# One more pair of output tiles as seven products in three places of a hybrid decoder layer

## The chip, the cores and the metric

The kernel runs on one core of a Trainium2 chip. A core has five engines, each with an instruction queue of its own that it works off in order: TensorE (PE, matrix products into PSUM, with PEld for the loading of its stationary operand), VectorE (DVE), ScalarE (ACT), GpSimd (POOL) and SyncE (SP, which here issues the DMAs). The engines run beside one another and wait for one another by semaphores. The metric is the device time of one execution in microseconds, and of several runs the median. A lower time is better.

## The reference

One layer step for 512 prompt tokens, 32 new tokens of running sequences and 16 meta tokens (560 columns in all; 544 once the meta tokens have done their part), width 1024, FFN width 2816:

```python
h = x + 0.5 * rms_norm(swiglu(rms_norm(x, ffn1_pre_g), ffn1_w_gate, ffn1_w_up, ffn1_w_down), ffn1_post_g)
u = rms_norm(h, mix_pre_g)
q_a, k_a, v_a, gk_low, r_a, q_b, k_b, v_b, gate_a, gate_b = jnp.split(u @ w_in, offs, axis=-1)
o_a = rms_norm(gla(q_a, k_a, v_a, gk_low), gla_norm_g) * jax.nn.silu(r_a)
o_b = stick_breaking_attention(q_b, k_b, v_b, sb_bias)
m = jax.nn.sigmoid(gate_a) * (o_a @ w_o_gla) + jax.nn.sigmoid(gate_b) * (o_b @ w_o_sb)
h = h + rms_norm(m @ w_out, mix_post_g)
y = h + 0.5 * rms_norm(swiglu(rms_norm(h, ffn2_pre_g), ffn2_w_gate, ffn2_w_up, ffn2_w_down), ffn2_post_g)
```

with `swiglu(x, g, u, d) = (silu(x @ g) * (x @ u)) @ d`, all in float32.

## The kernel before, in words

Everything lies feature-major: a tile has 128 features on the partitions and the tokens along the row, in two halves of 280 columns (272 once the meta tokens are gone). The 1024 features are 8 depth tiles, the 2816 of the FFN 22.

**A product in three matmuls.** Each float32 operand is split in two parts of fp32r: `hi`, a cast on ACT (`S.copy`), and `lo`, the value less `hi`, a subtraction on DVE (`tt` with `ALU.subtract`, whose instructions all carry line 166). A depth tile of a product is then hi times hi, hi times lo and lo times hi, for each half: 6 matmuls. A tile of 8 depth tiles takes 48.

**Seven products in place of eight.** Two output tiles over eight depth tiles, with two halves of columns, are a 2 x 2 by 2 x 2 product of quarters. They are also computed as seven products (PLAN and MIXER call such a pair "S" and a plain tile "R"): 7 x 4 x 3 = 84 matmuls in place of 96. For this DVE makes four sums of weight quarters (`weight_sums`, four of 128x512) and splits the quarters and sums of weights in four parts (`parts_of`, `parted_lo`: b1, t and b2 of 128x1024, t4 of 128x512), and four sums of activations s1 to s4 for each k of 0 to 3 (four instructions of half a row each), which are split as well; afterwards some adds put the seven results together. `seven_steps` does this for the mixer, `Down.pair` for the FFN's down projections.

**The order.** PE, DVE, ACT and POOL have a written-out order. `step()` marks every six matmuls, and `later(n, f)` puts `f` behind the n-th step from here on its engine's queue; `when` does so with steps counted from a pair's start. Nothing in that fixes a time: it fixes who stands behind whom. SP's order is a scheduler's. The rooms in SBUF are given out by the table PLACES, one byte for each `take`.

**FFN and down projection.** In the FFN (lines 1075 to 1306) gate and up are computed for tile f = 0 to 21; `hidden` splits the product of the two in `hi` and `lo` for the down projection. Tiles up to `late` are split as they come; from LATE (8) on they wait unsplit in `waiting`, and are split in every second step after the FFN's last matmul. Then follows the down projection, class `Down` and the loop over `by_chunks(order)`. Before, output tiles 0 and 1 are computed plainly, by turns in three chunks of depth (0 to 7, 8 to 14, 15 to 21), 44 steps and 264 matmuls in all. Then come the pairs 2 and 4: each plainly over the depth tiles 8 to 21 (`CUTS`, 28 steps, 168 matmuls, L1391 to L1394), and over the depth tiles 0 to 7 as seven products (84 matmuls, L1430 to L1432), the results being added to the plain ones. Tiles 6 and 7 follow plainly, one half after the other. For the activation sums `joined` puts `hi` and `lo` of depth tile i and i + 4 together again, `summed` makes s1 to s4, `sums_hi` and `sums_lo` split them; `pieces` queues all this for i = 0 to 3 from step DSUMS[0] on, every DSUMS[1] steps.

**The mixer's r gate.** `chain` runs the mixer's products by the table MIXER, its first ones beside the last pairs of heads of the attention. r has eight tiles: r 0, 1, 2 and 7 plain (`gate_r`, a tile of eight depth tiles in `tile_steps`, L699 to L702), then the pairs 3 and 5 as seven products (`r_pair`). `sums_back`, `sums_hi` and `sums_lo` make the activation sums for the mixer's pairs, at the steps SUMS_BACK; `whole_u` adds `hi` and `lo` of u for this, `halved` gives back rooms that only plain tiles need, and `out_a` is the product with w_o_gla, whose first tile names its depth order as the o tiles come ready.

Of the kernel before, what the change touches and what calls it, by code (L numbers as in the profile page):

```python
# [35 lines left out]
LATE1, LATE2 = 8, 8  # L36
# [20 lines left out]
6806666991008264690078680607082491770776681c069186424e3e343a74546e7266323c00368c4468767c2840781e6c820c0238708c762a2e
26927c8a040660622a2c4816246527702e1262186071152c622a2b2d6415712c1262632a622a2b2d642c71626306180c1e62714b71246a003254
883e64604b38020434308a6058763c786222122a482e4c4a8e2c7b84668c687e7f406056464f3d333579036b366e747044426c7215015939318b
7782893f055514157a804e5a7e825c2483284e655e92647c508d3a521e148c822667648466616764656766422c7016604668746c6e647244206a  # L60
0a6612088a6c1804343c8c780688916a761a720f026e22320e1c103057565584641486544000760c676a6c8a7248082e604c1a3e582a910e2c66
301c856e001257421002685655542040164675150c8a146a0a300e121e188c782a2c007074107620060421863442736c6e728988846475668e0c
17343e12324c4a42460b7476486a3c1c3004436e20080972621a3736876660860a436c8417686e8e6a642c1488568c430408063c906394708417
6664606c6e78728e8a68846a86606e17708468646a6c7894728e668a0c866e606c176478686a848e728a66706e6c866072177084026836646a6c
8e00786686948a6e401c6620721a1e178a646030948e106c0c6a0e181c2068708486366e786a4072102a221e20170094667038840e1a6e8e0c1c
60724068641c8a1e1a186c220260206e8e59540e2a0c84721e302e68100066606c94641e3840202200706694308e8464606e4740721002682e0e
# [68 lines left out]
def hybrid_step(  # L135
# [570 lines left out]
    def k_steps(acc, parts, k0, k1, kt, act, halves, nw=P, wid=(HW, HW)):  # L706
        hi, lo = parts
        for k in range(k0, k1):
# [15 lines left out]

    def step():

        arena.now += 1
        n = 0
# [2021 lines left out]
```

## Time and profile before

| | before |
|---|---|
| median of 3 runs | 1492.89 us (1492.89 to 1494.05) |
| the profiled execution | 1493.21 us |
| its span | 1491.2 us |
| granted clock of PE | 0.999 |
| PE instructions, matmuls and transposes | 11909 |
| DVE, ACT, POOL busy | 1106.0, 783.1, 68.4 us |
| DMA | 181.97 MB, mean 122 GB/s |

The span goes from the first to the last instruction that the profile shows; the execution's own time has 2.0 us besides. Times in the trace count from the span's start. A matmul row lists the modelled end, so that successive rows overlap: one of 128x280 is listed with 0.29 us, and the next starts 0.13 later.

The stages by the trace: FFN1's gate and up to 266.35, its down projection to 401, projections and GLA to 580, attention to 820, the mixer from 806 to 1056, w_out to 1143, FFN2's gate and up to 1347.95, its down projection to 1480, and the end.

### The profile page before, as it was taken

Reading aid. Unit: us, or ns where it says so; the run is one execution under the profiler, and the core shown is the slowest. Engines: PE = TensorE matmul, PEld = TensorE weight load, DVE = VectorE, ACT = ScalarE, POOL = GpSimd, SP = SyncE. Lnnn points to the kernel's source line nnn. Section 1 sums busy time; section 2 is a strip of 40 time slices with the busy share of each in tenths; the row PEclk is TensorE's granted clock in tenths of the full one; section 3 lists DMA queues with packets and bytes.
Section 4 is the critical chain, followed back from the end, with each engine's and each line's share of the span. In section 5 each row is a group of like instructions: output and inputs, shape, how many; then the busy total and the mean of one; then the engine's idle time right before and its main releaser. Section 6 shows DMA issues by size and latency. Waiting matters only on the chain.

```text
span 1491.2 us, 29865 instructions
## 1 busy us (share of the span) xinstructions
PE 1482.6 (99%) x11909; PEld 1435.2 (96%) x11909; DVE 1106.0 (74%) x1945; ACT 783.1 (53%) x1453; POOL 68.4 (5%) x145
## 2 busy tenths in 40 slices
PE   9999999999999999999999999999999999999998
PEld 8999999999999899999998999999999999999998
DVE  5888888855677866877887845777567898888544
ACT  7455454533555656566666543634564455455333
POOL 2000000000000011112111000000000000000000
PEclk9999999999999999999999999999999999999999
DMA  8133333324665584336555866344531333333253
GB/s 253 50 92 100 100 96 92 97 79 123 172 153 138 148 151 100 86 95 161 125 112 160 228 162 200 96 110 140 155 111 52 100 100 100 99 107 92 79 152 115
DMA packets 277230, 181.97 MB, mean 122 GB/s; under 512 B 10429, under 2 KB 255363, under 8 KB 277091
## 3 DMA queue, kind: packets, MB, share of 16 engines
q1 hardware_dynamic: 276786, 180.00, 44.7%
q8 instruction: 93, 1.52, 0.4%
q14 instruction: 47, 0.38, 0.1%
q0 software_dynamic: 288, 0.07, 0.0%
q10 hardware_dynamic: 16, 0.00, 0.0%
HBM read 155.06 MB, written 24.97 MB: 121 GB/s over the span
## 4 chain that ended last, share of the span: by engine, by line
PE 96%; DVE 2%; ACT 1%; DMA 1%; issue 0%; DVEq 0%; ACTq 0%
PE acc L1266 8%; PE acc L1267 8%; PE acc L1268 8%; PE acc L699 7%; PE acc L700 7%; PE acc L702 7%; PE acc L712 6%; PE acc L715 6%; PE acc L713 6%; PE acc L1046 2%; PE acc L1047 2%; PE acc L1048 2%; PE acc L1209 2%; PE acc L1206 2%; PE acc L1207 2%; PE ps L2041 1%
## 5 line engine op out<-in xcount | busy, mean ns | idle before, releaser
L166 DVE TENSOR_TENSOR room<-room,room 128x544 f32<-128x544 f32 (+18 forms) x457 | 285.6, 648 | 72.3 <-ACT room L779 16.7
L166 DVE TENSOR_TENSOR lo<-raw,hi 128x1024 fp32r<-128x1024 f32 (+1 forms) x207 | 248.1, 1199 | 105.5 <-ACT hi L678 66.7
L1266 PE MATMUL acc<-room,hi 128*128 128x280 f32 (+1 forms) x896 | 260.0, 290 | 0.0
L1268 PE MATMUL acc<-room,lo 128*128 128x280 f32 (+1 forms) x896 | 259.6, 290 | 0.0
L1267 PE MATMUL acc<-room,hi 128*128 128x280 f32 (+1 forms) x896 | 259.4, 289 | 0.0
L699 PE MATMUL acc<-room,hi 128*128 128x280 f32 x832 | 241.1, 307 | 0.2 <-DVE room L169 0.2
L700 PE MATMUL acc<-room,hi 128*128 128x280 f32 x832 | 225.0, 289 | 0.0
L977 ACT CAST hi<-raw 128x1024 fp32r<-128x1024 f32 x100 | 104.8, 1052 | 146.2 <-PE acc L1267 48.6
L702 PE MATMUL acc<-room,lo 128*128 128x280 f32 x832 | 173.1, 289 | 0.0
L1267 PEld LDWEIGHTS acc<-room,hi 128*128 128x128 f32 x896 | 168.9, 188 | 0.0
L1266 PEld LDWEIGHTS acc<-room,hi 128*128 128x128 f32 x896 | 168.8, 188 | 0.0
L1268 PEld LDWEIGHTS acc<-room,lo 128*128 128x128 f32 x896 | 168.6, 188 | 0.0
L699 PEld LDWEIGHTS acc<-room,hi 128*128 128x128 f32 x832 | 156.8, 188 | 10.1 <-issue 8.1
L700 PEld LDWEIGHTS acc<-room,hi 128*128 128x128 f32 x832 | 157.2, 189 | 1.2
L678 ACT CAST hi<-raw 128x1024 fp32r<-128x1024 f32 (+1 forms) x107 | 108.2, 1013 | 75.2 <-issue 21.5
L702 PEld LDWEIGHTS acc<-room,lo 128*128 128x128 f32 x832 | 130.3, 189 | 0.0
L977 ACT CAST hi<-room 128x1024 fp32r<-128x1024 f32 x92 | 76.9, 836 | 87.3 <-PE acc L1267 58.5
L166 DVE TENSOR_TENSOR lo<-room,hi 128x1024 fp32r<-128x1024 f32 x92 | 87.9, 955 | 43.4 <-ACT hi L977 43.0
L712 PE MATMUL acc<-room,hi 128*128 128x280 f32 (+2 forms) x388 | 110.8, 295 | 0.0
L713 PE MATMUL acc<-room,hi 128*128 128x280 f32 (+2 forms) x388 | 108.9, 290 | 0.0
L166 DVE TENSOR_TENSOR room<-room,acc 128x272 f32<-128x272 f32 (+1 forms) x180 | 76.2, 437 | 43.8 <-PE acc L1048 20.9
L712 PE MATMUL acc<-room,room 128*128 128x280 f32 (+3 forms) x364 | 107.4, 295 | 0.0
(397 smaller groups left out, 3437.2 us busy)
## 6 DMA issues: line engine op xcount, KB each, us to landing
raw<-in_w_in_dram SPq DMA_DIRECT2D x43, 512.0 KB, 7.2
raw<-in_ffn_w_gate_dram SPq DMA_DIRECT2D x64, 256.0 KB, 3.1
raw<-in_ffn_w_up_dram SPq DMA_DIRECT2D x64, 256.0 KB, 3.4
raw<-in_ffn_w_down_dram SPq DMA_DIRECT2D x36, 448.0 KB, 3.9
raw<-in_w_in_dram SPq DMA_DIRECT2D x40, 256.0 KB, 4.7
out_dram<-room SPq DMA_DIRECT2D x36, 256.0 KB, 3.7
room<-in_cache_k_dram SPq DMA_DIRECT2D x32, 256.0 KB, 5.7
room<-in_cache_v_dram SPq DMA_DIRECT2D x32, 256.0 KB, 4.7
```

Source lines behind the costliest of these rows:

```text
L166: (eng or V).tensor_tensor(out=out, in0=a, in1=b, op=op)
L678: S.copy(h_, src)
L699: T.matmul(acc[h][:, : wid[h]], hi[k], a[h][0], start=(k == order[0]), stop=False)
L700: T.matmul(acc[h][:, : wid[h]], hi[k], a[h][1], start=False, stop=False)
L702: T.matmul(acc[h][:, : wid[h]], lo[k], a[h][0], start=False, stop=(k == order[-1]))
L712: T.matmul(acc[h][:nw, : wid[h]], wh, a[h][0], start=(k == 0), stop=False)
L713: T.matmul(acc[h][:nw, : wid[h]], wh, a[h][1], start=False, stop=False)
L715: T.matmul(acc[h][:nw, : wid[h]], wl, a[h][0], start=False, stop=(k == kt - 1))
L977: S.copy(hi[:, :kt], src)
L1266: T.matmul(x[:, :QW], hi, act[k][0], start=(first and k == 0), stop=False, skip_group_check=True)
L1267: T.matmul(x[:, :QW], hi, act[k][1], start=False, stop=False, skip_group_check=True)
L1268: T.matmul(x[:, :QW], lo, act[k][0], start=False, stop=(k == 3), skip_group_check=True)
```

## The change

In each down projection the tiles 0 and 1 are no longer computed plainly: pair 0 is done as the pairs 2 and 4 are. In all three pairs the plain part is now over the depth tiles 0 to 13 (`CUTS`) and the seven products over 14 to 21 (`S0` = 14), the last eight that the FFN makes. The tiles from 14 on are kept unsplit until they have been summed, so that `joined` goes: `summed` reads them from `hid.wait`, `parted` splits them at the side, `given` gives their rooms back. `first` splits the tiles 12 and 13, LATE goes from 8 to 12, so that 8 to 11 are split inside the FFN, and the activation sums start at step 1, every 6 steps, in place of 14 and 8. The seven products now begin 28 steps after the projection's first matmul; before it was 44 + 28.

In the mixer the plain r tiles 2 and 7 go, and r is 0 and 1 plain, then the pairs 2, 4 and 6. SUMS_BACK, `halved` and the depth order of the first `out_a` follow. `um.full` has another layout for k below 4, which costs `whole_u` one add more. PSUM tags are exchanged, and PLACES is a new table, of which one line each is shown. In the whole program PE has 36 matmuls fewer, DVE 25 instructions more, ACT 11 and SP 6 DMAs.

```diff
-LATE1, LATE2 = 8, 8
+LATE1, LATE2 = 12, 12
...
-SUMS_BACK = (-85, -61, -37, -20)
-MIXER = [("R", "r", 0), ("R", "r", 1), ("R", "r", 2), ("R", "r", 7), ("S", "r", 3), ("S", "r", 5)]
+SUMS_BACK = (-80, -62, -44, -27)
+MIXER = [("R", "r", 0), ("R", "r", 1), ("S", "r", 2), ("S", "r", 4), ("S", "r", 6)]
...
-UNITS, LONGS = 150, 16
+UNITS, LONGS = 150, 17
...
-0c060018121e242a7094908082848668766a5066565e5c787c5452724e7a5836221c884c8c6c3064484a6e60613a2e8a3e446236923c465a3036
...
-24363d3440243a3e243865268202906c626e70
+5a0630002c121e1a688019527c8c905082787e886a3e6094724c6e644a8e76542a7a408448243626286c928a8b16046270863c0c8a5874563642
...
-    DSUMS1, DSUMS2 = (14, 8), (14, 8)
+    DSUMS1, DSUMS2 = (1, 6), (1, 6)
...
     def step():
...
-    def hidden(f, sl, at, nw, wid, hid, pairs):
+    def hidden(f, sl, at, nw, wid, hid, pairs, held=False):
...
-            give(sl)
+            if not held:
+                give(sl)
...
-        waiting = []
+        waiting = hid.wait = {}
...
         def hidden_or_wait(f, sl, at):
...
-                waiting.append((f, sl))
+                waiting[f] = sl
...
-                if not sums and "S" not in plan[f - RE_FFN :] and n % 2 == 0 and waiting:
-                    hidden(*waiting.pop(0), 1, nw, wid, hid, pairs)
...
-        for i in range(len(waiting) + 3):
-            later(2 * i + 1, lambda: waiting and hidden(*waiting.pop(0), 1, nw, wid, hid, pairs))
-
...
     class Down:
...
-        CUTS = ((8, 15), (15, 22))
-
-        def __init__(self, hid, nw, nm):
+        CUTS, S0 = ((0, 7), (7, 14)), 14
+
+        def __init__(self, hid, nw, nm, pairs=None):
+            self.pairs = pairs
...
-            return plain + [((a, b), 0, KD, 0, P, "quarters"), ((b, a), 4 * P, KD, 0, P, "quarters")]
-
-        def joined(self, i, m):
-            hi, lo = self.hid.full[i + 4 * m]
-            self.r[i, m] = t = take(NT)
-            tt(t[:, : self.nw], hi[:, : self.nw].bitcast(F32), lo[:, : self.nw].bitcast(F32), ALU.add)
+            return plain + [((a, b), cls.S0 * P, KD, 0, P, "quarters"), ((b, a), cls.S0 * P + 4 * P, KD, 0, P, "quarters")]
+
+        def parted(self, i):
+            for f in (self.S0 + i, self.S0 + i + 4):
+                hidden(f, self.hid.wait[f], 1, self.nw, None, self.hid, self.pairs, True)
+
+        def first(self):
+            for n, f in enumerate(sorted(f for f in self.hid.wait if f < self.S0)):
+                hidden(f, self.hid.wait.pop(f), 2 + 4 * n, self.nw, None, self.hid, self.pairs)
...
         def summed(self, i):
...
-            x, y = self.r.pop((i, 0)), self.r.pop((i, 1))
+            x, y = (self.hid.wait[f] for f in (self.S0 + i, self.S0 + i + 4))
...
-            give(x, y)
+
+        def given(self, i):
+            give(*(self.hid.wait.pop(f) for f in (self.S0 + i, self.S0 + i + 4)))
...
         def pieces(self, start, every):
+            self.first()
...
-                for d, f in ((0, lambda i=i: self.joined(i, 0)), (1, lambda i=i: self.joined(i, 1)), (2, lambda i=i: self.summed(i)),
-                             (4, lambda i=i: self.sums_hi(i, 0)), (5, lambda i=i: self.sums_hi(i, 1)),
-                             (6, lambda i=i: self.sums_lo(i, 0)), (7, lambda i=i: self.sums_lo(i, 1))):
+                for d, f in ((0, lambda i=i: self.parted(i)), (1, lambda i=i: self.summed(i)),
+                             (3, lambda i=i: self.sums_hi(i, 0)), (4, lambda i=i: self.sums_hi(i, 1)), (4, lambda i=i: self.given(i)),
+                             (5, lambda i=i: self.sums_lo(i, 0)), (6, lambda i=i: self.sums_lo(i, 1))):
...
-                            T.matmul(acc[i, h][:, :w], hi[k - k0], a, start=(k == 8), stop=False, skip_group_check=True)
+                            T.matmul(acc[i, h][:, :w], hi[k - k0], a, start=(k == 0), stop=False, skip_group_check=True)
...
-                                     stop=((i, h, k) == (n + 1, 1, KF - 1)), skip_group_check=True)
+                                     stop=((i, h, k) == (n + 1, 1, self.S0 - 1)), skip_group_check=True)
...
-            a11, a12, a22 = ([hid.t[k0 + k, h] for k in range(4)] for h, k0 in ((0, 0), (0, 4), (1, 4)))
+            a11, a12, a22 = ([hid.t[self.S0 + k0 + k, h] for k in range(4)] for h, k0 in ((0, 0), (0, 4), (1, 4)))
...
-    order1 = [(0, (0, 1)), (1, (0, 1)), "S2", "S4"] + [(n, (0,)) for n in range(6, 8)] + [(n, (1,)) for n in range(7, 5, -1)]
...
+    order1 = ["S0", "S2", "S4"] + [(n, (0,)) for n in range(6, 8)] + [(n, (1,)) for n in range(7, 5, -1)]
...
-        r = [(n, hs, j) for j in range(3) for n, hs in order[:2]]
-        for t in order[2:]:
+        r = []
+        for t in order:
...
-                um.full[k] = take(NT, F32R), take(NT, F32R)
+                um.full[k] = a, b = take(NT, F32R), take(NT, F32R)
...
-                    um.t[k, i] = um.full[k][0][:, cs[i]], um.full[k][1][:, cs[i]]
+                    um.t[k, i] = ((a, b)[i][:, :HW], (a, b)[i][:, HW:]) if k < 4 else (a[:, cs[i]], b[:, cs[i]])
...
         def whole_u(i):
...
-            for t, k in ((x, i), (y, i + 4)):
-                hi, lo = um.full[k]
-                tt(t[:, :NW], hi[:, :NW].bitcast(F32), lo[:, :NW].bitcast(F32), ALU.add)
+            for h in range(2):
+                hi, lo = um.get(i, h, W2[h])
+                tt(x[:, h * HW : h * HW + W2[h]], hi.bitcast(F32), lo.bitcast(F32), ALU.add)
+            hi, lo = um.full[i + 4]
+            tt(y[:, :NW], hi[:, :NW].bitcast(F32), lo[:, :NW].bitcast(F32), ALU.add)
...
-                usum["a", h, k] = um.full[k][0][:, c], um.full[k][1][:, c]
+                usum["a", h, k] = um.get(k, 0, QW) if k < 4 else tuple(t[:, c] for t in um.full[k])
...
     def out_a(n):
-        acc = yield from tile_steps(oas, W1, (0, 1, 2, 7, 3, 4, 6, 5) if n == 0 else range(KD))
+        acc = yield from tile_steps(oas, W1, (0, 1, 2, 3, 4, 5, 7, 6) if n == 0 else range(KD))
...
         def halved():
...
-                parts_ = [arena.halves(t) for t in um.full[k]]
-                give(*(t[1] for t in parts_))
-                um.full[k] = [t[0] for t in parts_]
-
-        when(starts["r", 3], halved)
+                give(um.full[k][1])
+                um.full[k] = um.full[k][:1]
+
+        when(starts["r", 2] + 1, halved)
...
```

On DVE, in FFN1's down projection before the change: the last instructions ahead of the `lo` of the first weights of seven products (the last row, of pair 2). `lo253` and `lo255` are parts of plain weights, `raw248` and `raw254` the quarters, `room42` and `room98` their sums.

```order
L166 TENSOR_TENSOR lo253_3551<-raw244_3363,hi253_3550 128x896
L166 TENSOR_TENSOR lo255_3607<-raw246_3427,hi255_3606 128x896
L166 TENSOR_TENSOR room42_72_3356<-raw254_3553,raw248_3484 128x512
L166 TENSOR_TENSOR raw248_3484<-raw248_3484 128x512
L166 TENSOR_TENSOR room42_72_3356<-raw254_3553,raw248_3484 128x512
L166 TENSOR_TENSOR room98_50_886<-raw254_3553,room42_72_3356 128x512
L166 TENSOR_TENSOR lo257_3707<-raw248_3484,hi257_3706 128x1024
```

The same place after the change, now in pair 0 (`raw232` and `raw238` are the quarters, the rows of 128x560 the splitting of tiles 14 to 21 and of the sums, those of 128x280 the activation sums):

```order
L166 TENSOR_TENSOR raw232_3158<-raw232_3158 128x512
L166 TENSOR_TENSOR room66_76_3326<-room0_4_69,room66_76_3326 128x560
L166 TENSOR_TENSOR room48_77_3342<-raw238_3176,raw232_3158 128x512
L166 TENSOR_TENSOR room48_77_3342<-room24_8_73,room0_4_69 128x280
L166 TENSOR_TENSOR room136_73_3256<-room24_8_73 128x280
L166 TENSOR_TENSOR room48_77_3342<-room48_77_3342,room24_8_73 128x280
L166 TENSOR_TENSOR room136_73_3256<-room0_4_69,room48_77_3342 128x280
L166 TENSOR_TENSOR room30_78_3343<-raw238_3176,room48_77_3342 128x512
L166 TENSOR_TENSOR room102_79_3353<-room24_8_73,room60_20_150 128x560
L166 TENSOR_TENSOR room106_81_3355<-room0_4_69,room104_80_3354 128x560
L166 TENSOR_TENSOR lo241_3387<-raw232_3158,hi241_3386 128x1024
```

The seven rows of before are all the weights'. After, the activations' sums and subtractions stand between the weights' sums, ahead of that `lo` in the same queue.

On DVE, beside the attention's last pairs of heads before the change (rows of 128x544 belong to the attention, to r's gate and to the o tiles, `L2028` copies scores from PSUM, `lo731` is a plain r tile's weights):

```order
L166 TENSOR_TENSOR room112_162_8692<-room112_162_8692,room104_169_9154 128x544
L2028 COPY room12_155_8316<-ps732_9549 128x512
L166 TENSOR_TENSOR room132_177_9524<-room100_174_9421,room104_176_9523 128x544
L166 TENSOR_TENSOR room136_179_9547<-room112_162_8692,room140_178_9546 128x544
L2028 COPY room18_75_3493<-ps734_9566 128x384
L166 TENSOR_TENSOR lo731_9538<-raw688_8998,hi731_9537 128x1024
L2028 COPY room84_127_6627<-ps735_9578 128x384
L166 TENSOR_TENSOR room144_128_6721<-ps736_9583,room144_128_6721 32x512
```

And after it (`raw694` and `raw705` are quarters of the weights of r pair 2, `lo736` is its first part):

```order
L166 TENSOR_TENSOR room96_103_5288<-raw705_9156,raw694_9002 128x512
L166 TENSOR_TENSOR room116_151_8022<-raw705_9156,room96_103_5288 128x512
L166 TENSOR_TENSOR room6_87_4524<-room6_87_4524,ps730_9444 128x512
L166 TENSOR_TENSOR room148_168_9488<-room60_107_5437,room106_167_9487 128x544
L166 TENSOR_TENSOR room138_112_5521<-acc722_9356,room138_112_5521 128x280
L166 TENSOR_TENSOR room138_112_5521<-acc723_9357,room138_112_5521 128x264
L166 TENSOR_TENSOR room36_84_4285<-room36_84_4285,room138_112_5521 128x544
L166 TENSOR_TENSOR lo736_9539<-raw694_9002,hi736_9538 128x1024
L2033 COPY room0_4_69<-ps739_9565 128x512
L166 TENSOR_TENSOR room138_170_9563<-room36_84_4285,room114_169_9562 128x544
L2033 COPY room124_166_9442<-ps740_9578 128x384
L2033 COPY room18_106_5366<-ps741_9589 128x384
```

Where one plain tile's `lo` stood among the attention's instructions, weight sums and the `lo` of the pair's parts stand there now.

More of the change, by code (lines that the diff above doesn't have):

```diff
@@ L57 @@
[L57 to L66, printed above, removed]
@@ new lines @@
+50427278797f461a71547e00907078797c04721a7073797802467d087291187c78421d00701c7d7c9044181a7279787c060a70007c1879711c1a
+720690187873707c1800721d091c78061d0070081c18900879781c1d0200181d74787270908a2e4a92686a360c761448128866247c6c2c7a6804
+4230204066686a3488064e1f881c333018201e8923008823041f011a050033888900880501041f020388233624420c00238923037a7e4c4a8a40
+8822099016823e726834863c7814480010080a2092221e0633944e7c2a6f6e12605c6c0d4b3f878341736a70768c625a645e03158b793d694d84
+7f7b89910c1c3466182c6e0532581c3084188e2e1b50541c2a4e0c0e185256957c02946c6d181c6d18766a8c705e605a9464046c1a7c6268143a
@@ L79 @@
+71706b6c0471068a6b6a7e0e7270006e6d6c717e0e8b06708a6d6c947e6e006a6f6c6d8a946f06706d686c026e6a6b0300068a68706a6c303254
+1e008e36185c34667a1412247c945e90740c06001640728e7810142a6e0d100c11007e0f0e0c10131516750c12171474121675158b74148a8a75
+241218382a36066e0a742a8a2e74074e68446c66082c6a
 """)
@@ L1644, in hybrid_step @@
             if hs is None:
-                down1.pair(n, ("ps", "acc") if n == 2 else ("acc", "ps"), n == 4)
+                down1.pair(n, ("acc", "ps") if n == 2 else ("ps", "acc"), n == 4)
                 if n == 4:
@@ L1649, in hybrid_step @@
             if j == 0:
-                accs[n, hs] = {h: ps("ps" if (n, hs) == (6, (0,)) else "acc") for h in hs}
+                accs[n, hs] = {h: ps("acc") for h in hs}
             acc, (k0, k1) = accs[n, hs], CUTS[j]
@@ L2671, in hybrid_step @@
         nd, last, accs = Last(half2, NW // 2), {}, {}
-        down2 = Down(hid, NW, nd)
+        down2 = Down(hid, NW, nd, pairs)
         down2.pieces(*DSUMS2)
@@ L2688, in hybrid_step @@
             if hs is None:
-                down2.pair(n, ("ps", "acc") if n == 2 else ("acc", "ps"), n == 4)
+                down2.pair(n, ("acc", "ps") if n == 2 else ("ps", "acc"), n == 4)
                 if n == 4:
@@ L2693, in hybrid_step @@
             if j == 0:
-                accs[n, hs] = {h: ps("ps" if (n, hs) == (6, (0,)) else "acc") for h in hs}
+                accs[n, hs] = {h: ps("acc") for h in hs}
             acc, (k0, k1) = accs[n, hs], CUTS[j]
```

33 lines of the change are left out of this document (18 added, 15 removed).

## The prediction

> **What bounds the kernel now.** The page comes first: busy time by engine, the slices of the granted clock, the chain that ended last.
>
> ```profile
> PE 1482.6 (99%) x11909; PEld 1435.2 (96%) x11909; DVE 1106.0 (74%) x1945; ACT 783.1 (53%) x1453; POOL 68.4 (5%) x145
> PEclk9999999999999999999999999999999999999999
> PE 96%; DVE 2%; ACT 1%; DMA 1%; issue 0%; DVEq 0%; ACTq 0%
> ```
>
> PE is busy 99% of the span, at full clock, and carries 96% of the chain. So a matmul taken out is worth its whole time, and anything else costs only where PE comes to wait. The list of PE's waits shows how little of that there is:
>
> ```profile
> PE acc L715 <- DVE lo L166: 0.6, 1, 0.6
> PE ps L2244 <- DVE room L2214: 0.4, 1, 0.4
> ```
>
> So two questions remain: how many matmuls go, and where PE meets an engine that is late. The engine to watch is DVE. In these stretches of the windows view (columns: window, length, then busy us and count of PE, PEld, DVE, ACT, POOL, then clock, DMA share, GB/s) it is full, or near it:
>
> ```profile
> 285.00:290.00 5.00, 5.00 (x41) 5.00 (x40) 4.97 (x9) 2.89 (x6) 0.00 (x0) 1.00 0.02 1
> 805.00:835.00 30.00, 29.58 (x316) 26.47 (x318) 24.96 (x63) 17.07 (x35) 2.60 (x6) 1.00 0.65 174
> ```
>
> The first lies in FFN1's down projection just after its start at 266.35, the second in the attention's tail, where the mixer's first r products run. The change touches both.
>
> **Part 1: matmuls that go.** PE alone, by windows:
>
> ```profile
> 266.35:300.34 33.99, 33.99 (x267) 1.00 0.31 88
> 300.34:332.76 32.42, 32.42 (x255) 1.00 0.26 76
> 1347.95:1381.07 33.12, 33.12 (x267) 1.00 0.33 92
> 1381.07:1412.67 31.60, 31.60 (x254) 1.00 0.27 78
> 966.00:978.09 12.09, 12.09 (x99) 1.00 0.41 105
> 978.09:988.62 10.53, 10.53 (x87) 1.00 0.41 115
> ```
>
> In each couple the first row is a pair done as two plain tiles, the second a pair with quarters: the down tiles 0 and 1 (264 matmuls) and pair 2 (252) of FFN1, the same of FFN2, and in the mixer two plain tiles (96) and a pair of seven products (84); the counts hold two or three border matmuls. Pair 0 of either down projection and one r pair pass from the first kind to the second: 1.57 + 1.52 + 1.56 = 4.65 us less. Nothing that PE does takes their place: the joining of hi and lo and all sums are DVE's.
>
> **Part 2: the new wait in pair 0 of each down projection.** Before, the seven products of a down projection began 72 steps after its start, and used the depth tiles 0 to 7, finished long ago. Now pair 0 comes first, its seven products begin after 28 steps, and they use the depth tiles 14 to 21, the last that the FFN makes. The time that PE gives, and the time that DVE needs, both start at the projection's first matmul:
>
> ```profile
> 266.35 0.29 PE L712 MATMUL acc<-room,hi 128*128 128x280 f32 x1
> 266.55 0.45 DVE L166 TENSOR_TENSOR room<-room,acc 128x280 f32<-128x280 f32 x1 [0.89 <-PE acc L1268]
> 300.34:321.94 21.60, 21.60 (x171) 21.60 (x169) 9.77 (x13) 5.52 (x10) 0.00 (x0) 1.00 0.31 92
> 321.94 0.29 PE L1430 MATMUL acc<-room,hi 128*128 128x280 f32 x1
> 1381.07:1402.15 21.08, 21.08 (x170) 21.08 (x169) 9.94 (x13) 5.56 (x10) 0.00 (x0) 1.00 0.33 95
> ```
>
> Twenty-eight steps take 21.60 us (pair 2, up to its first product at 321.94), 21.08 in FFN2. The weights' `lo` is first read by the third product matmul, 0.25 later: due at 21.85 and 21.33.
>
> DVE cannot run ahead of the FFN: its last output add waits for PE's last FFN matmul and starts 0.20 after the projection has begun. From that add to the `lo` there are 42 DVE instructions in the changed order, counted from it: 17 of 128x280 (that add, and four groups of four activation sums), 17 of 128x560 (the last tile's product, 2 `lo` for depth tiles 12 and 13, 8 for 14 to 21, 6 `lo` of sums), 3 of 128x896 (`lo` of plain weights), 4 of 128x512 (weight sums) and the 128x1024 itself. Durations overlap from one instruction to the next, so I price from start to start:
>
> ```profile
> 281.00 4.65 DVE L166 TENSOR_TENSOR room<-room,room 128x560 fp32r<-128x560 f32 x7
> 298.12 0.45 DVE L166 TENSOR_TENSOR room<-room,room 128x280 f32<-128x280 f32 x1
> 298.48 0.80 DVE L166 TENSOR_TENSOR room<-room 128x280 f32<-128x280 f32 x2
> 299.32 0.45 DVE L166 TENSOR_TENSOR room<-room,room 128x280 f32<-128x280 f32 x1
> 299.69 1.08 DVE L166 TENSOR_TENSOR lo<-raw,hi 128x896 fp32r<-128x896 f32 x1
> 300.69 0.73 DVE L166 TENSOR_TENSOR room<-room,room 128x560 fp32r<-128x560 f32 x1
> 821.29 1.22 DVE L166 TENSOR_TENSOR lo<-raw,hi 128x1024 fp32r<-128x1024 f32 x1
> 822.43 0.68 DVE L166 TENSOR_TENSOR room<-raw,raw 128x512 f32<-128x512 f32 x1
> 823.15 0.69 DVE L166 TENSOR_TENSOR raw<-raw 128x512 f32<-128x512 f32 x1
> 1362.29 3.26 DVE L166 TENSOR_TENSOR room<-room,room 128x544 fp32r<-128x544 f32 x5
> 1378.29 0.72 DVE L166 TENSOR_TENSOR room<-room,room 128x544 f32<-128x544 f32 x1
> 1379.04 1.62 DVE L166 TENSOR_TENSOR room<-room 128x272 f32<-128x272 f32 x4
> 1380.58 1.08 DVE L166 TENSOR_TENSOR lo<-raw,hi 128x896 fp32r<-128x896 f32 x1
> ```
>
> Seven of 128x560 in 4.65 are 0.652 apart ((4.65 - 0.73) / 6). A group of four of 128x280 takes 299.69 - 298.12 = 1.57, its first 0.36. A 128x896 takes 300.69 - 299.69 = 1.00. A 128x512 takes 0.72 and less; I take 0.64. So FFN1: 0.20 + 0.36 + 4 x 1.57 + 17 x 0.652 + 3 x 1.00 + 4 x 0.64 + 1.22 = 24.70 us. PE stands from 21.85: **a wait of 2.8**. FFN2 has 0.635 ((3.26 - 0.72) / 4) and 1.54 (1380.58 - 1379.04): 24.3 against 21.33, **a wait of 3.0**. Together +5.8, which is more than part 1 saves. [...] A piece of the wait may show earlier, at a product's first matmul waiting for ACT's `hi`, since the casts stand behind sums that DVE makes; the total is the same.
>
> Ends: were DVE a tenth quicker than counted, both waits would be about 0.4; at whole durations the sum goes the other way (a rival below). The later products ask for their `lo` 24 matmuls apart, about 3 us, and each costs DVE 1.2, so the first wait is the only one.
>
> **Part 3: what moves into the FFN.** Tiles 8 to 11 are now split as they come (four casts, four subtractions of 0.65 on DVE). There is room:
>
> ```profile
> 150.00:170.00 20.00, 20.00 (x158) 20.00 (x157) 17.01 (x27) 9.57 (x14) 0.00 (x0) 1.00 0.37 105
> ```
>
> DVE leaves 3 us free in 20, PE waits for nothing: cost 0. The eight joining adds that go (8 x 0.65) are already out of the count of part 2.
>
> **Part 4: the third r pair.** It puts on DVE, in the attention's tail, four weight sums (4 x 0.69), three `lo` of 1.22 and one of 0.68, for one tile's `lo` of 1.22: 2.76 + 3.66 + 0.68 - 1.22 = 5.9 us more where 30.00 - 24.96 = 5.04 are free. If all that free time can be used, 0.9 is late. But much of it is one hole:
>
> ```profile
> 820.65 0.73 DVE L166 TENSOR_TENSOR room<-room,room 128x544 fp32r<-128x544 f32 x1 [3.22 <-ACT room L2281]
> ```
>
> If those 3.22 stay a wait for ACT, 0.9 + 3.2 = 4.1 is late. Downward, PE's 0.4 at L2244 may go with the new order. I take **+0.7** between -0.4 and +4.1, nearer the low end, since the new work does not read that result of ACT and so can stand ahead of the wait.
>
> **Part 5: the rest.** PE's one other loss in a stage that changes is in FFN1's last down tiles:
>
> ```profile
> 376.90 0.29 PE L713 MATMUL acc<-room,hi 128*128 128x280 f32 x1
> 377.79 0.40 PE L715 MATMUL acc<-room,lo 128*128 128x280 f32 x1 [0.60 <-DVE lo L166]
> ```
>
> Weights land late there, behind other loads; SP's order there now has one load in place of another, so I let it stand: 0, between -0.8 and +0.8. The PSUM tags, the third add in `whole_u`, and the k order of `out_a` put nothing on PE: 0. The loads of the down weights (KB each, median us to landing):
>
> ```profile
> raw<-in_ffn_w_down_dram SPq DMA_DIRECT2D x36, 448.0 KB, 3.9
> ```
>
> Pair 0's quarters are asked for about 11 steps (11 x 21.60 / 28 = 8.5 us) ahead of their sums, and land in 3.9: hidden, with over 4 us to spare.
>
> **Sum.** 1493.21 (profiled execution) - 4.65 + 5.8 + 0.7 = 1495.06. That execution stands 0.32 above the median of the runs, 1492.89. So **1494.7**. What a measurement of this kernel can tell from no change is 0.2%, 3.0 us: the band is 1489.9 to 1495.9.
>
> **Rivals.**
> *Forecast* (0.60): waits of 2 to 3.5 in each pair 0, r between 0 and +1.5: 1492.5 to 1496.
>
> *Slower: the attention's tail* (0.22). DVE's hole at 820.65 stays, and the r pair's `lo` come 4.1 late instead of 0.7: 1498.1. It decides against "same" from 1.2 us above my r term (1495.9 - 1494.7). For it: DVE is an in-order queue, 25 of 30 us full. Against: the hole is 3.2 wide and PE's wait there was only 0.4.
>
> *Slower: durations add* (0.05). If DVE starts an instruction only when the one before has left, the queue of FFN1 is 0.20 + 17 x 0.45 + 17 x 0.73 + 3 x 1.08 + 4 x 0.69 + 1.22 = 27.5, the wait 5.6; FFN2's 27.3, with 0.72 for the 0.73, and 6.0: +5.8 over the forecast, 1500.5. The seven rows that take 4.65, not 5.11, speak against it; one group of mixed shapes could still run so. [...]
>
> *Slower: the clock* (0.05). A stall near 3 us could make PE restart at a lower clock. The trace has no such stall in mid-run; after the 0.6 at 377.79 the rate went on at 1.00, and only at the end, with PE idle from 1485.05 + 1.16, is the clock lower:
>
> ```profile
> 372.00:378.00 6.00, 5.40 (x42) 5.17 (x41) 1.22 (x2) 1.69 (x2) 0.00 (x0) 1.00 1.01 276
> 1485.05 1.16 PE L843 MATMUL acc<-ident,room 128*32 128x128 f32 x8 [0.42 <-DVE room L166]
> 1486.00:1491.00 5.00, 0.21 (x2) 0.00 (x0) 1.08 (x2) 0.82 (x2) 0.00 (x0) 0.86 0.39 135
> ```
>
> If the lower clock followed each stall for as long as the stall lasted, at half rate, PE would lose another 1.4 and 1.5: +2.9, 1497.6. [...]
>
> *Faster* (0.08). DVE keeps up in pair 0 and the tail costs nothing: 1493.21 - 4.65 - 0.32 = 1488.2; it takes both waits together under 1.65. For it: casts and subtractions need not all stand where I count them busy. Against: at 285 to 290 the same kinds of instruction left DVE no gap.
>
> That the change doesn't do what it says is out: the changed program has 36 matmuls fewer, 12 for each of three pairs.
>
> **Chances.** Above 1495.9: the three slower rivals, 0.32, less what of them is small, plus the forecast's upper edge: 0.32. Below 1489.9: 0.08. Between: 0.60. Low end 1490.5: waits of half my size, and some luck in the tail; high end 1499.0: above the tail rival and the clock rival, and short of "durations add".
>
> **What would show it.** In the changed profile: the two down windows with 252 matmuls in 32.4 plus a wait of 2.8 and 31.6 plus 3.0; PE's wait list with `lo` or `hi` ahead of the first product at L1433 to L1435, DVE gapless for 24 us there; three r pairs of 10.5 us, and PE's waits at 805 to 835 under 1.5. I am wrong if PE's list shows no wait of over 1 us in pair 0 (my DVE sum is too long), or if the tail holds more than 2 us of it.

## The result, and the profile after

The changed kernel takes 1497.87 us (median of 8 runs, 1496.97 to 1500.51) against 1492.89 for the kernel before (8 runs, 1492.22 to 1494.05). The ratio is 1.0034, with an interval of 1.0025 to 1.0043: slower by a third of a per cent. A second set of runs of the same two kernels gave 1.0027 (1.0016 to 1.0038). The profiled execution took 1497.98 us, its span 1496.3.

The page of the changed kernel, engines and chain:

```profile
PE 1482.2 (99%) x11873; PEld 1433.9 (96%) x11873; DVE 1114.7 (74%) x1970; ACT 790.5 (53%) x1464; POOL 70.4 (5%) x145
PE 92%; DVE 5%; DMA 1%; ACT 1%; issue 1%; DVEq 0%; ACTq 0%; SPq 0%
```

PE has 36 instructions fewer, and yet it is busy 0.4 us less only. Four per cent of the chain have gone from PE to others, 3 of them to DVE. The waits of PE:

```profile
PE acc L1435 <- DVE lo L166: 2.7, 2, 1.4
PE acc L1433 <- ACT hi L978: 2.2, 2, 1.2
...
PE ps L2249 <- DVE room L2219: 0.4, 1, 0.4
```

The first two rows are new: two times each, once in each down projection. Here is the first of these places, PE and then DVE:

```profile
290.70 0.40 PE L1433 MATMUL acc<-room,hi 128*128 128x280 f32 x1 [0.98 <-ACT hi L978]
...
292.58 0.60 PE L1435 MATMUL acc<-room,lo 128*128 128x280 f32 x1 [1.36 <-DVE lo L166]
292.98 0.43 PE L1433 MATMUL acc<-room,hi 128*128 128x280 f32 x1
293.22 0.43 PE L1434 MATMUL acc<-room,hi 128*128 128x280 f32 x1
```

```profile
268.07 0.45 DVE L166 TENSOR_TENSOR room<-room,acc 128x280 f32<-128x280 f32 x1 [0.90 <-PE acc L1269]
291.31 1.22 DVE L166 TENSOR_TENSOR lo<-raw,hi 128x1024 fp32r<-128x1024 f32 x1
```

The projection began at 267.87. The third product matmul, the first to read the weights' `lo`, began at 292.58, 24.71 us later; the forecast's time without a wait is 21.85. After it the matmuls are listed with 0.43 and start 0.23 apart, where they had been 0.13 apart. The windows show why (length, PE's busy time and count, granted clock, DMA share, GB/s). The first two rows are pair 0's plain part and its seven products in FFN1, the next two are neighbouring stretches of 3.41 us in there, and the last two are the two parts of pair 0 in FFN2:

```profile
267.87:290.70 22.83, 21.85 (x171) 1.00 0.24 72
290.70:304.64 13.94, 12.58 (x85) 0.88 0.23 67
288.85:292.26 3.41, 1.40 (x9) 1.00 0.00 0
292.26:295.67 3.41, 3.08 (x13) 0.50 0.45 133
1351.65:1374.09 22.44, 21.20 (x170) 1.00 0.26 77
1374.09:1386.32 12.23, 10.89 (x85) 1.00 0.26 77
```

For 3.41 us, from 292.26 to 295.67 and so most of them after the wait, PE had half its clock. In FFN2, after the same wait, it had all of it.

Elsewhere, the attention's tail (the window of before, 5 us later), first of the changed kernel in all engines; then the FFNs' 16 blocks of seven products and, in the middle row, the part of the mixer with the r pairs, PE alone, of the kernel before and of the changed one:

```profile
809.90:839.90 30.00, 29.63 (x316) 26.53 (x319) 29.50 (x71) 18.01 (x36) 2.04 (x5) 1.00 0.68 189
```

```profile
93.44:266.35 172.91, 172.91 (x1346) 1.00 0.34 99
890.67:944.93 54.26, 54.26 (x592) 1.00 0.65 181
1179.52:1347.95 168.43, 168.43 (x1347) 1.00 0.35 101
```

```profile
94.63:267.87 173.24, 173.24 (x1347) 1.00 0.34 98
895.53:948.15 52.62, 52.62 (x580) 1.00 0.59 152
1182.69:1351.65 168.96, 168.96 (x1346) 1.00 0.35 101
```

DVE fills 29.50 of 30 us in the tail, and PE's one wait there is the 0.4 that it was before: the new work went into the idle time to the last half microsecond. The r pair is worth 54.26 - 52.62 = 1.64 us. The FFNs, where no matmul was added, take 0.33 and 0.53 more.

Stage by stage, in us against the kernel before, of the profile above and of a second pair of profiles (`e_again` against `e_before`):

| stage | forecast | first pair | second pair |
|---|---|---|---|
| up to FFN1's seven products | 0 | +1.19 | +0.44 |
| FFN1, 16 blocks | 0 | +0.33 | +0.33 |
| down 1, pair 0 | -1.57 + 2.85 | +2.78 | +1.38 |
| down 1, pairs 2 and 4 | 0 | +0.17 | +0.18 |
| down 1, first halves of tiles 6 and 7 | 0 | +0.46 | +1.12 |
| mixer with the r pairs | -1.56 + 0.7 | -1.64 | -1.62 |
| FFN2, 16 blocks | 0 | +0.53 | +0.53 |
| down 2, pair 0 | -1.52 + 2.97 | +1.55 | +1.56 |
| all the rest | 0 | -0.3 | -0.1 |
| end of the span | +1.9 | +5.1 | +3.9 |

### The profile page after: what moved, and what is told of

Its sections match the earlier page's. It is cut to its first block, busy times and chain, and to the rows that moved or that the text cites. A ratio compares the mean times of both kernels' runs of the same rounds, so it can differ in the third digit from the quotient of the medians.

```text
span 1496.3 us, 29817 instructions
## 1 busy us (share of the span) xinstructions
PE 1482.2 (99%) x11873; PEld 1433.9 (96%) x11873; DVE 1114.7 (74%) x1970; ACT 790.5 (53%) x1464; POOL 70.4 (5%) x145
## 3 DMA queue, kind: packets, MB, share of 16 engines
q8 instruction: 93, 1.52, 0.4%
## 4 chain that ended last, share of the span: by engine, by line
PE 92%; DVE 5%; DMA 1%; ACT 1%; issue 1%; DVEq 0%; ACTq 0%; SPq 0%
PE acc L1268 8%; PE acc L1269 8%; PE acc L1267 8%; PE acc L699 7%; PE acc L702 7%; PE acc L700 7%; PE acc L712 5%; PE acc L715 5%; PE acc L713 5%; DVE room L166 3%; PE acc L1047 3%; PE acc L1048 2%; PE acc L1049 2%; PE acc L1207 2%; PE acc L1210 2%; PE acc L1208 2%
## 5 line engine op out<-in xcount | busy, mean ns | idle before, releaser
L166 DVE TENSOR_TENSOR room<-room,room 128x272 f32<-128x272 f32 (+16 forms) x439 | 269.5, 631 | 60.8 <-ACT room L779 9.9
L1269 PE MATMUL acc<-room,lo 128*128 128x280 f32 (+1 forms) x896 | 259.8, 290 | 0.0
L1267 PE MATMUL acc<-room,hi 128*128 128x280 f32 (+1 forms) x896 | 259.6, 290 | 0.0
L1268 PE MATMUL acc<-room,hi 128*128 128x280 f32 (+1 forms) x896 | 259.6, 290 | 0.0
L699 PE MATMUL acc<-room,hi 128*128 128x280 f32 (+1 forms) x800 | 231.5, 306 | 0.2 <-DVE room L169 0.2
L700 PE MATMUL acc<-room,hi 128*128 128x280 f32 (+1 forms) x800 | 216.1, 289 | 0.0
L978 ACT CAST hi<-raw 128x1024 fp32r<-128x1024 f32 x106 | 111.0, 1051 | 143.4 <-PE acc L1268 54.6
L1267 PEld LDWEIGHTS acc<-room,hi 128*128 128x128 f32 x896 | 168.6, 188 | 0.0
L1268 PEld LDWEIGHTS acc<-room,hi 128*128 128x128 f32 x896 | 168.6, 188 | 0.0
L1269 PEld LDWEIGHTS acc<-room,lo 128*128 128x128 f32 x896 | 168.4, 188 | 0.0
L702 PE MATMUL acc<-room,lo 128*128 128x280 f32 (+1 forms) x800 | 166.5, 289 | 0.0
L699 PEld LDWEIGHTS acc<-room,hi 128*128 128x128 f32 x800 | 150.6, 188 | 9.9 <-issue 7.9
L700 PEld LDWEIGHTS acc<-room,hi 128*128 128x128 f32 x800 | 150.9, 189 | 1.2
L678 ACT CAST hi<-raw 128x1024 fp32r<-128x1024 f32 (+1 forms) x101 | 102.1, 1010 | 63.2 <-issue 10.8
L166 DVE TENSOR_TENSOR lo<-room,hi 128x1024 fp32r<-128x1024 f32 x98 | 93.5, 954 | 45.5 <-ACT hi L978 45.0
L702 PEld LDWEIGHTS acc<-room,lo 128*128 128x128 f32 x800 | 125.2, 188 | 0.0
L978 ACT CAST hi<-room 128x1024 fp32r<-128x1024 f32 x98 | 81.8, 835 | 80.4 <-PE acc L1268 45.7
L712 PE MATMUL acc<-room,room 128*128 128x280 f32 (+3 forms) x362 | 106.8, 295 | 0.0
L713 PE MATMUL acc<-room,room 128*128 128x280 f32 (+3 forms) x359 | 103.9, 289 | 0.0
L715 PE MATMUL acc<-room,room 128*128 128x280 f32 (+3 forms) x357 | 103.4, 290 | 0.1
```

The source lines that it names most:

```text
L166: (eng or V).tensor_tensor(out=out, in0=a, in1=b, op=op)
L678: S.copy(h_, src)
L699: T.matmul(acc[h][:, : wid[h]], hi[k], a[h][0], start=(k == order[0]), stop=False)
L700: T.matmul(acc[h][:, : wid[h]], hi[k], a[h][1], start=False, stop=False)
L702: T.matmul(acc[h][:, : wid[h]], lo[k], a[h][0], start=False, stop=(k == order[-1]))
L712: T.matmul(acc[h][:nw, : wid[h]], wh, a[h][0], start=(k == 0), stop=False)
```

## Experiments

**The changed kernel and the kernel before once more** (`e_again`, `e_before`), unedited.

> The changed kernel once more, for what is steady in its profile. Theory: pair 0's first lo 24.7 us after each down projection's start and waits of 2.8 to 3.1 are steady; the half-rate stretch, which followed the wait in FFN1 and not in FFN2, depends on how the idle time lies against a window of the clock's control and may come after either, both or none (1.4 us each); the 1.2 us lost before FFN1's seven products is chance and may be 0 to 1.2. Rival: the stretch belongs to FFN1, and the first 1.2 us to the new rooms, and both return.

> The kernel before once more, for what is steady in its profile. Theory: its blocks of 84 matmuls take 10.81 and 10.53 again, while the time up to FFN1's seven products (93.44) and the first halves of tiles 6 and 7 (20.17), in which PE waits on loads, come out up to 1 us longer, as in the other kernels. Rival: both are its own and return to 0.1, so that the change costs 0.5 to 1.2 us at these two places.

The changed kernel gave 1496.66 (7 runs, 1496.45 to 1498.52), the kernel before 1492.79 in the one run of `e_before` (the median of 20 other runs beside it is 1493.25). Pair 0 in both down projections:

```profile
267.45:290.28 22.83, 21.85 (x170) 1.00 0.25 75
290.28:302.82 12.54, 11.18 (x84) 1.00 0.26 75
1350.05:1372.49 22.44, 21.20 (x171) 1.00 0.25 75
1372.49:1384.73 12.24, 10.90 (x85) 1.00 0.28 77
```

The waits are the same to 0.01 us: pair 0 without them would take 32.42 and 31.60, so they are 35.37 - 32.42 = 2.95 and 34.68 - 31.60 = 3.08. The half rate did not come back: 12.54 in place of 13.94. So the 1.40 comes and goes, and the wait does not. In the kernel before the FFN blocks came out the same:

```profile
93.77:266.68 172.91, 172.91 (x1347) 1.00 0.34 99
365.50:385.18 19.68, 19.55 (x150) 1.00 0.87 259
1179.39:1347.82 168.43, 168.43 (x1346) 1.00 0.35 101
```

The +0.33 and +0.53 belong to the program. Where PE waits on loads, in the second row (20.17 in the first profile), the kernel before varies by half a microsecond and the changed one (20.62, then 20.80) was longer both times; the start varies too.

**The waits filled** (`e_fill`): 22 matmuls whose result is thrown away, ahead of pair 0's first product, in both down projections.

```diff
             a, d, b, c = (ps(tags[1]) for _ in range(4))
+            if n == 0:
+                for j in range(22):
+                    T.matmul(a[:, :w], hid.t[0, 0][0][:, :P], hid.t[1, 0][0][:, :w], start=True, stop=True, skip_group_check=True)
```

> The changed kernel with 22 useless matmuls (22 x 0.1285 = 2.83 us) on PE between pair 0's plain part and its first product, in both down projections; each writes the bank that the first product then starts afresh. They fill the time in which PE would wait, and take no work from DVE. Theory, idle PE lowers its clock: the first product's lo comes when it did, so the waits are filled, not shortened, but no stretch at half rate follows in FFN1's pair 0 (about 1.4 us in the changed kernel's profile): 1496.5, and the runs lie closer together than 3.5 us. Rival, the slow stretch has another cause (the loads and the casts that begin there): it stays, with 24 matmuls 0.23 apart, and the time is 1497.9 or, as the fill makes nothing shorter, a little more.

1497.31 (8 runs, 1496.51 to 1498.53), ratio 1.0028 (1.0018 to 1.0039), 0.8 above the theory; in its profile 0.7 was lost at a load in tile 6. Pair 0 in FFN1 took 24.53 and 10.87, 35.40 together, as with the wait (35.37), with no half rate:

```profile
267.44:291.97 24.53, 24.53 (x193) 1.00 0.23 67
291.97:302.84 10.87, 10.87 (x87) 1.00 0.30 87
```

PE's own work takes the place of the wait and the end does not move, so the `lo` does not depend on what PE does. On the clock this run decides nothing, since `e_again` had no half rate either; the next two runs do.

**The wait made longer** (`e_more`), **and filled** (`e_morefill`, that edit and the one above with 43).

```diff
         def rest():
-            tt(lo[:, :nw], sl[:, :nw], hi[:, :nw].bitcast(F32), ALU.subtract)
+            for _ in range(2 if held and f < 18 else 1):
+                tt(lo[:, :nw], sl[:, :nw], hi[:, :nw].bitcast(F32), ALU.subtract)
```

> The changed kernel with four subtractions of pair 0 (the lo of tiles 14 to 17) done twice, 4 x 0.65 = 2.6 us more on DVE ahead of the first lo, in both down projections. Theory, DVE's queue is the wait and a long enough idle time of PE brings the half rate for certain: waits of 5.5 and 5.7 in place of 2.9 and 3.1, a half-rate stretch after both: 1496.7 + 5.2 + 2 x 1.4 = 1504.7, and 1501.9 if no stretch follows. Rival, DVE has slack there and the wait is set elsewhere: no change, 1496.7.

> The kernel with the four doubled subtractions, and 43 useless matmuls (43 x 0.1285 = 5.5 us) ahead of pair 0's first product, in both down projections, so that PE works through the time that it would wait. Theory, the half rate in the kernel with the doubled subtractions comes from PE's idle time: the first lo comes when it did, but no matmul is 0.23 apart, and the time is 1496.7 + 2 x 2.6 = 1501.9, 3.9 below that kernel's 1505.8. Rival, it comes from what the other engines do at that place: the half-rate stretches stay, 1505.8.

`e_more`: 1505.77 (4 runs within 0.41), ratio 1.0081 (1.0065 to 1.0097). `e_morefill`: 1503.04 (4 runs within 0.61), ratio 1.0064 (1.0048 to 1.0079). First `e_more`, pair 0 of FFN1 and of FFN2, then the clock, twice in FFN1 and once in FFN2:

```profile
267.42:292.59 25.17, 21.86 (x171) 1.00 0.22 66
292.59:308.00 15.41, 13.27 (x85) 0.78 0.21 61
1355.01:1379.71 24.70, 21.19 (x170) 0.98 0.23 69
1379.71:1394.04 14.33, 12.53 (x85) 0.80 0.23 65
289.64:293.06 3.42, 0.47 (x2) 1.00 0.00 0
293.06:299.88 6.82, 4.68 (x21) 0.50 0.24 68
1375.08:1378.50 3.42, 1.12 (x9) 1.00 0.00 0
```

and `e_morefill` at FFN1's pair 0:

```profile
295.41 0.40 PE L1439 MATMUL acc<-room,lo 128*128 128x280 f32 x1 [0.18 <-DVE lo L166]
295.64 0.29 PE L1437 MATMUL acc<-room,hi 128*128 128x280 f32 x1
```

Four subtractions more in DVE's queue put the first `lo` matmul at 27.83 us after the start, not 24.71. That is 3.1 later, where I had 2.6: a repetition cost 0.78, not 0.65. In the trace it starts 0.77 after the first, which is listed with 0.73, and so only when the first, whose output it overwrites, has ended; unrelated ones start 0.65 apart. With 43 useless matmuls ahead of it, the `lo` matmul starts at 27.84 (295.41 - 267.57): the same `lo`, at the same time, but the clock stays at 1.00; only the first step behind the short wait is 0.23, and from there on the matmuls are 0.13 apart. In `e_more` the half rate comes in both down projections. So it is PE's idleness that lowers its clock: keeping PE busy with nothing saves 2.7 us in all. That is less than the 3.9 that I had; pair 0 alone gained 2.1 and 1.3, and 0.7 was lost again at a load in tile 6.

When the clock drops is not set by the program alone. In the trace of the changed kernel the half clock lasts 3.413 us, and the times at which the granted clock changes lie whole multiples of that apart: from 295.67 to its drop at the end, 1493.75, the changed kernel has 1198.08, which is 351 of them, and the two drops of `e_more`, 293.06 and 1378.49, are 1085.43 apart, which is 318. Counted back from the drop at the end, this grid lies differently against the program from one execution to the next: from the start of FFN1's down projection to the step at pair 0's wait it is 20.98 us in the first profile, 22.91 in `e_again` and 21.26 in `e_rooms`. Here is the step of it in which PE worked least around pair 0's wait, in four places: FFN2 of the changed kernel, FFN1 and FFN2 of `e_again`, and FFN1 of `e_rooms`, a run described below.

```profile
1374.29:1377.70 3.41, 2.07 (x16) 1.00 0.12 36
290.36:293.77 3.41, 2.05 (x14) 1.00 0.09 29
1372.39:1375.80 3.41, 1.97 (x13) 1.00 0.11 16
288.95:292.36 3.41, 1.12 (x7) 1.00 0.00 0
```

Behind the first three, with 1.97 us of PE work or more, the clock stayed full. Behind the last, and behind the steps with 1.40, 0.47 and 1.12 shown before, it was halved, for one step (3.41) or two (6.82), until a step with 2.99 us of work or more had passed (3.08 in the changed kernel, 2.99 in FFN2 of `e_more`). In the traces of the kernel before and of the changed one no step goes against this: ahead of the drop at the end PE worked 0.04 and 1.16 us, and in every other whole step but the one with 1.40 it worked 2.07 or more. So a step with 1.40 us of work in it was idle enough, and whether the wait of 2.9 brought the half rate went by how it fell on the grid, which differed from one execution to the next.

**The same work in another order** (`e_best`, `e_best2`, `e_best3`). Nothing is left out; only the steps of pair 0's instructions change. The last of the three:

```diff
-                for d, f in ((0, lambda i=i: self.parted(i)), (1, lambda i=i: self.summed(i)),
...
+                for d, f in zip(((0, 1, 3, 4, 4, 5, 6), (0, 1, 3, 4, 4, 5, 13), (0, 3, 4, 5, 10, 6, 8))[max(0, i - 1)], (
...
+    FIRST = (((-10, -10, -7, 1)), (("b1", -9, -7), ("t", -6, -3), ("b2", -2, 0), ("t4", 4, 6)))
+    OTHER = ((-10, -10, -9, -8), (("b1", -6, -5), ("t", -2, -1), ("b2", 0, 1), ("t4", 4, 6)))
...
-            weights_at(when, 28, key)
-            for d in (-5, -1):
+            weights_at(when, 28, key, FIRST if n == 0 else OTHER)
+            for d in (-5 if n else -11, -1):
```

and, of tiles 17 and 21 (the last to be split), the `lo` of the first comes two steps sooner, that of the second six steps later. `e_best` has t at (-4, -2), b2 at (0, 1), t4 at (2, 5), the fourth weight sum at -1, no 13 in the first line (a 6, as in the row ahead of it), and -5 for the -11; `e_best2` has t4 at (3, 5), and -5.

> The changed kernel with pair 0's DVE and ACT work in another order: the weights' b1 right after the two weight sums it needs, the split of tile 17 ahead of it, the third and fourth weight sums, the second half of the activation sums' lo and the split of tile 21 behind it, each ahead of its own product. Not one instruction less. Theory, DVE's queue ahead of the first lo is the wait: that lo now has some 35 instructions ahead of it, not 41, and comes before PE asks; later ones are due at most 0.3 late: both waits (2.9 and 3.1) fall below 0.6, the half-rate stretch goes, 1497.9 - 5.2 - 1.4 = 1491.3, a little below the kernel before. Rival, what PE waits for there is set by something else (ACT's casts, a weight load): the wait only moves to another operand, and the time stays at 1496 or above.

1493.49 (11 runs within 0.69), ratio 1.0002 (0.9993 to 1.0011). The first wait is gone (21.69 in FFN1, as without one); what is left in FFN1 is 1.5 us (12.33 for 10.83) at the third product:

```profile
292.00 0.40 PE L1440 MATMUL acc<-room,hi 128*128 128x280 f32 x1 [0.20 <-ACT hi L981]
...
293.26 0.40 PE L1442 MATMUL acc<-room,lo 128*128 128x280 f32 x1 [0.74 <-DVE lo L166]
```

```profile
291.98 1.23 DVE L166 TENSOR_TENSOR lo<-room,hi 128x1024 fp32r<-128x1024 f32 x1 [0.77 <-ACT hi L981]
```

I had 0.3 for it, because I had left ACT out: t's cast stood behind two casts of sums that DVE makes, and DVE then waited 0.77 for it.

> The reordered kernel with t's cast on ACT ahead of the casts of the last two activation sums, t's lo ahead of the lo of s3 and s4 for k = 2 and 3, b2's lo ahead of tile 21's, and the fourth weight sum last. The instructions are the same. Theory, order on DVE and ACT is all that is left of the wait: t's lo, which came 1.3 us late, is now ready when its product asks, so pair 0 takes 32.5 in FFN1 and 31.6 in FFN2, the whole down change is then worth its matmuls: 1493.5 - 1.5 - 1.8 = 1490.2, below the kernel before by 0.2%. Rival, DVE's total work up to the products is the limit, whatever its order: the wait moves on to the next part (b2 or s3), and the time stays within 0.5 of 1493.5.

1492.77 (11 runs, 1492.33 to 1493.56), ratio 0.9996 (0.9986 to 1.0005). Pair 0 is free of waits (10.83 in FFN1), but 0.94 of the 1.50 won there shows up in pair 2, whose plain part takes 22.63 for 21.69:

```profile
299.75 1.08 DVE L166 TENSOR_TENSOR lo<-raw,hi 128x896 fp32r<-128x896 f32 x1
300.88 0.40 PE L1404 MATMUL acc<-room,lo 128*128 128x280 f32 x1 [0.66 <-DVE lo L166]
```

The `lo` of pair 2's plain weights stood behind output adds, which wait for PE's products.

> The second reordered kernel with the split of pair 2's first plain weights ten steps before the end of pair 0 in place of five, so that their lo stands ahead of t4's and of the output adds, which wait for PE; t4 one step later. In the second reordered kernel pair 0 had no wait, but pair 2's first plain lo came 0.94 and 1.05 us late behind those adds. Theory, again only order: that wait goes too, pair 2's plain part takes 21.7 and 21.05, the time 1492.8 - 2.0 = 1490.8, below the kernel before by 0.15%. Rival, DVE has no time left there and the wait goes to t4 or to tile 3's weights: 1492.8.

1490.67 (11 runs, 1490.02 to 1490.88), ratio 0.9980 (0.9971 to 0.9989): below both kernels.

```profile
267.49:289.18 21.69, 21.69 (x170) 1.00 0.26 76
289.18:300.02 10.84, 10.84 (x86) 1.00 0.38 112
300.02:321.71 21.69, 21.69 (x170) 1.00 0.35 100
```

No wait is left in pair 0 or 2 of FFN1; in FFN2 one `lo` still costs pair 0 some 0.4 (10.92 for 10.56). The rival (DVE's work as such is too much) fell: the same instructions fit.

**The r part alone** (`e_r`): the kernel before with the change's lines on MIXER, SUMS_BACK, `um.full`, `whole_u`, `halved` and `out_a`, and rooms of my own.

```diff
-MIXER = [("R", "r", 0), ("R", "r", 1), ("R", "r", 2), ("R", "r", 7), ("S", "r", 3), ("S", "r", 5)]
+MIXER = [("R", "r", 0), ("R", "r", 1), ("S", "r", 2), ("S", "r", 4), ("S", "r", 6)]
...
```

> The kernel before with the change in the mixer alone: r as 0, 1 and the pairs 2, 4, 6, with SUMS_BACK, whole_u, halved and the depth order that go with it; the down projections as before, rooms by a table of its own. Theory, the r pair is worth its matmuls and the attention's tail hides its DVE work: 1.6 us less, 1491.3. Rival, the tail does not hide it: 1.6 less and 0.7 to 4.1 more, 1492.0 to 1495.4, with PE waits between 805 and 865 us that the kernel before does not have.

1493.81 (11 runs, 1493.18 to 1496.06), ratio 1.0005 (0.9996 to 1.0015). That is 2.5 above the theory, but not where the rival has it:

```profile
93.64:267.51 173.87, 173.87 (x1347) 1.00 0.34 99
893.25:945.91 52.66, 52.66 (x580) 1.00 0.57 152
```

The r stage takes 52.66, 1.6 less than before, and PE's waits in the tail are as they were. The loss is in FFN1 (173.87, +0.96) and in its down projection (+1.2, of which 0.9 in tiles 6 and 7, where PE waits on loads), whose PE, DVE and ACT instructions are those of the kernel before, in the same order, but whose rooms are others; its FFN2, also with other rooms, takes 168.43 as before. As a time of the r part the run is inconclusive; as a look at its stage it is clear.

**Other addresses** (`e_rooms`): every byte of PLACES moved on in its own kind of room.

> The changed kernel with the rooms turned round: every long room lies 7 long rooms further, every short one 14 short ones further, so who shares a room with whom, every wait and the order of all instructions are the same, and only the addresses differ. In the changed kernel a block of 84 matmuls in the FFNs takes 10.83 and 10.56 us, every one of the 16, where the kernel before has 10.81 and 10.53 (0.9 us in all). Theory, addresses set this: the blocks take another time than 10.83 and 10.56, the whole changes by up to 1 us. Rival, it is something else in the program: 10.83 and 10.56 again, 1496.7.

1497.97 (10 runs, 1496.46 to 1500.81), ratio 1.0030 (1.0020 to 1.0039). The FFN stages take 173.23 and 168.95, as in the changed kernel:

```profile
94.46:267.69 173.23, 173.23 (x1346) 1.00 0.34 98
1182.79:1351.74 168.95, 168.95 (x1346) 1.00 0.35 101
290.52:304.58 14.06, 12.69 (x84) 0.88 0.22 67
1374.18:1386.42 12.24, 10.89 (x84) 1.00 0.27 77
```

Moving all rooms by the same steps leaves the blocks' rate as it was: the theory fell in this form. It does not clear the rooms altogether, for `e_r`, with another table, has 10.87 in FFN1 (173.87 over 16) where the kernel before has 10.81. The last two rows have the half rate in FFN1 again and not in FFN2.

## Why the prediction was right or wrong

The measured time lies in the range of 1490.5 to 1499.0, but 3.2 above the 1494.7 in it, and for other reasons than those for which the upper end was put there.

**The matmuls that go: right.** Pair 0 as good as without waits takes 32.53 and 31.96 in `e_best3`, where I had 32.42 and 31.60, and the r stage is 1.64 and 1.62 shorter, where I had 1.56.

**The wait in pair 0: right, cause and size.** The queue of 42 instructions, priced from start to start, gave 24.70 us from the projection's start; the trace has 24.71. The waits are 2.95 and 3.08 for 2.85 and 2.97. The part that shows as a wait for ACT's `hi` is there too. `e_more` moved the wait with the queue, `e_fill` showed that it is not PE that sets it, and `e_best3` that the order of the queue is all there is to it. The rival "durations add", with 5.6 and 6.0, is out.

**The attention's tail: the work was there, the cost was not.** I took +0.7, because 5.9 us of DVE work met 5.04 of free time. It cost nothing: DVE's busy time there rose by 4.54 only, to 29.50 of 30 us, and PE waits as before.

**The clock: here the sum fails.** I gave the half rate 0.05, taking stalls of 2.8 and 3.0 as too short to bring it, which no run had shown. They are not too short: 1.40 us of work in 3.41 did not keep the clock up. The half rate came in FFN1's pair 0 of the first profile (1.40, as the rival had it) and of `e_rooms`, not in `e_again`, and in none of FFN2's. The mean granted clock of each run tells how common it was: a stretch of 3.41 us at half the clock takes 0.0011 off it, and of the 25 runs with that wait (`after`, `e_again`, `e_rooms`) 18 show 0.996 to 0.998 and 7 show 0.999, while the 33 runs of the three reordered kernels all show 0.999 or 1.000. (Two of the 11 runs of `e_r` show 0.998, and no profile was taken of these.) The runs at 0.999 took 1496.45 to 1497.16, the three at 0.996 took 1500.51 to 1500.81. It was a term with a chance of its own, between 0 and some 4 us, and should have been added to the forecast as such rather than set aside as a rival.

**"The rest", taken at nothing: too low by about 2 us.** The 16 blocks take 10.83 each for 10.81 in FFN1, 10.56 for 10.53 in FFN2 (173.24 and 168.96 over 16), in `e_again` and `e_rooms` as well: +0.86. Waits do not cause it, nor does a shift of all rooms; what does stays open, the choice of rooms included. Tiles 6 and 7, in which PE waits on late weights, were 0.5 and 1.1 longer, the start 1.2 and 0.4; of both a part is chance, as the two profiles of the kernel before show (20.17 and 19.68), and I can't say how much.

So the forecast of 1494.7 was 3.2 too low, with the wait in pair 0 right and the clock wrong: by the first profile it lacked the half rate (1.4), the blocks (0.9) and loads and start (1.6), against 0.7 too much for the tail. A change within 0.2% was the likelier side by my numbers, and it came out slower by a third of a per cent. What I called the likeliest way to get there, the tail, was not it.

## What to carry to other kernels

Putting a step with fewer matmuls first in a stage makes it meet the queue that the stage before has left on VectorE: count that queue from start to start, and ask what each operand's own due time is. Where the sum is late, order the queue by due time, with the casts on ScalarE that it waits for, before giving the change up: here the same instructions went from 0.3% slower to 0.2% faster. A stall of PE of about 3 us had a second price in two of six places here, 1.4 and 1.5 us, in the microseconds after it; filling a stall of 6 us with useless matmuls avoided that price (`e_morefill`, clock 1.00), ordering the queue avoided both (`e_best3`, 1490.67 us).

## What the runs showed of the hardware

The granted clock fell to 0.50 after 2.9 to 3.1 us of waiting that was broken by two matmuls, in two of six such places, and after about 6 us at both of two (`e_more`); it stayed there for 3.41 us or for 6.82, most of it with PE at work. The changes lie on a grid of 3.413 us (351 of them in 1198.08 us of the changed kernel, 318 in 1085.43 of `e_more`); of the steps measured, those in which PE was busy 1.40 us or less were followed by the half clock, those with 1.97 or more were not, and none lies between the two. A stretch of useless matmuls prevented it (`e_morefill`: 1.00 from 267.57 to 306.07). And a block of 84 matmuls of 128x280 without any wait took 10.81, 10.83 or 10.87 us, according to the program, and in each of its 16 repeats 10.80 to 10.81 in the kernel before and 10.82 to 10.84 in the changed one; a shift of all addresses changed nothing, another table of rooms, with the same matmuls in the same order, went with 10.87 in place of 10.81, and the cause is open.
